# Four prepared half tiles instead of three in the block phase of a hybrid decoder layer, with the forget gate kept in DRAM meanwhile

## The chip, the core and the metric

The kernel runs on one core of one Trainium2 chip. The metric is the device time of one execution in microseconds; the time before is the median of three runs. Engines are named as in the profile: PE is the matrix engine (PEld its weight loads), DVE the vector engine, ACT the scalar engine, POOL the GpSimd engine, SP the engine that here only issues DMAs. POOL also issues DMAs, on a queue of its own.

## What is computed

One decoder layer of width 2048 on 256 tokens. A normalised input is multiplied by one wide matrix, whose columns feed two mixers in parallel: a gated linear attention (GLA) with four heads and a differential attention with sixteen. Both outputs are gated, projected, merged and projected once more. Cut to what matters:

```
h = rmsnorm(x, pre_norm_g)
a_q, a_k, a_v, a_g, a_lr, b_q, b_k, b_v, b_g, m_a, m_b = split(h @ w_in)
gk  = log_sigmoid(a_lr @ gla_gk_w2 + gla_gk_b) / 16          # the forget gate
o_a = gla_chunked(a_q, a_k, a_v, gk)                          # needs gk
y_a = (rmsnorm(o_a) * silu(a_g)) @ w_branch_a
o_b = diff_attention(b_q, b_k, b_v, lam)
y_b = (0.8 * rmsnorm(o_b) * silu(b_g)) @ w_branch_b
x   = x + rmsnorm((sigmoid(m_a) * y_a + sigmoid(m_b) * y_b) @ w_out)
```

All of it is float32. A product of two float32 matrices is made of three products of rounded parts: each operand is split into a high part (rounded) and a low part (the rest), and hi by hi, hi by lo and lo by hi are summed.

## The kernel before, in words

**Half tiles.** The weights come from DRAM in the order in which they are used, and are taken in half tiles of 128 x 1024 values (4 KB a partition). For each half, `emit_half` (L339) makes two tiles: `hi`, a rounding copy by ACT (L371), and `lo`, the raw values minus hi, by DVE (L372). Both lie in a pool with three buffers each (`wpool`, L148, tags `hi` and `lo`). `take` (L380) hands the next pair to the matmuls, and first sees to it that the halves up to three further (`AHEAD`, L24) have been emitted. A tile of the fourth half from here takes the buffer of the present one, and so waits until PE has used it.

**The phase.** After the v columns 2 to 3 of GLA (`token_major`, L594) comes the phase (L920 to L931). Its order is written out by `phase_steps` (L102): ten block sets, of seven products each in the order `PRODUCTS` (1, 3, 2, 5, 6, 7, 4), and every product in four halves: 28 halves a set. A set is a 2 x 2 block product with seven multiplications instead of eight, so its weights are sums of blocks. Two blocks of each set are loaded into `chain` tiles (`link`, L222) and changed in place: DMAs on POOL's queue add blocks to them (L252), and DVE adds b or c to a (L260). The third kind of raw block, `c` (named `raws`), is loaded by SP into the big pool (L241, L242), four tiles a set. Between the products of a set lie partner halves of other weights (`PARTNERED`, L38, and four more in the first set): the last v columns, then q and k of GLA, then the first heads of the differential attention. A set's half is six matmuls for PE, a partner's half twelve or sixteen. PE's order in the phase is the program's own (`mm`, L578). SP's and POOL's DMAs are pinned to program order as well (`tc.keep_in_program_order`), while ACT and DVE instructions are ordered by the framework's planner.

**What leaves a product.** After product 6 and product 7 of a set DVE reads the bank into a tile `gr` (L901, L910, with raised priority), after 2 and 4 ACT writes a tile `gl` (L864, L868). Both are stored to DRAM by POOL (`spill`, L174) in the next set, at its product 3 (`SPILL_AT`, L40).

**The big pool.** `u` (L158) hands out its 18 buffers of 4 KB a partition (`BIG`, L42). In the phase it holds the eight tiles of the normalised input (`xs`, L390), the c tiles, gr and gl, a tile of q or k in the making, v tiles until they are stored, and the two tiles `gp` of the forget gate (L665). These are made while the v columns 2 and 3 are multiplied (`forget_gate`, L644; the last step is L687) and first read after the phase, in `gla_scores` (L944, the exponential at L967 of the profile). A buffer whose tile is stored comes free when the store has landed.

**The end of the phase.** When product 7 of the last set begins its second quarter, POOL fetches q and k of both halves back into the big pool (L927, L928). After the phase, the chain tiles' memory becomes a second pool (L934), and GLA is worked on beside the remaining heads.

## Time and profile before

| | |
|---|---|
| runs shown, median (lowest to highest) | 1079.25 us (1079.2 to 1079.81) |
| profiled execution | 1080.03 us |
| its span, first to last instruction | 1078.1 us |
| mean granted PE clock | 0.999 |
| DMA traffic | 295.54 MB, mean 274 GB/s |
| phase, from its first matmul to the end of the last set's partner | 81.3 to 633.9 us, and products 4 of the last set behind it |

The profile is of one execution. A row of a group of instructions gives the line of the kernel, the engine, the operation, what it writes and reads, its count, then the busy time and the mean of one in ns, then the idle time of the engine before them and what ended it. A row of the timeline gives start and duration in us, engine, line, operation, and in brackets the idle time just before it with its releaser. A row of a stretch gives its bounds, its length, the busy time of each engine (with the number of its instructions), PE's granted clock, the mean busy share of the 16 DMA engines and the GB/s. A row of waits reads: who waited, for whom, total us, times, longest. PE's end times are modelled, as matmuls overlap.

### The profile page before, as it was taken

The numbers are of one execution on the slowest core, as the hardware profiler recorded it, in microseconds if no ns is written. First come the engines' busy times: TensorE is split into PE (matmuls) and PEld (weight loads), VectorE is DVE, ScalarE is ACT, GpSimd is POOL, SyncE is SP. The second block draws the span as 40 slices with busy tenths as digits, with TensorE's granted clock in tenths as the row PEclk, the third lists the DMA queues.
The fourth block names the chain that finished last, engine by engine and source line by source line (L and its number), as shares of the span: only waits on it lengthen the run. The fifth ranks groups of instructions, "written<-read, shape, count | busy, mean of one in ns | idle before, by whom it ended". The sixth has DMA issues, their size and how long they took to land.

```text
span 1078.1 us, 15451 instructions
## 1 busy us (share of the span) xinstructions
PE 1066.4 (99%) x5380; PEld 914.4 (85%) x5380; DVE 959.7 (89%) x1273; ACT 765.3 (71%) x1122; POOL 179.6 (17%) x259
## 2 busy tenths in 40 slices
PE   9999999999999999999999999999999999999997
PEld 8998888888888888888888888898988888888886
DVE  7798999999999999999999989976877988889886
ACT  7897676777676767676767766765687887566662
POOL 0201121212121212121212211012111112100000
PEclk9999999999999999999999999999999999999999
DMA  9899798989898989999898867769989888988752
GB/s 349 271 352 310 194 339 259 322 230 320 224 324 215 310 245 335 284 273 303 267 298 262 206 231 279 253 206 310 334 282 305 264 269 273 346 303 257 271 192 99
DMA packets 68365, 295.54 MB, mean 274 GB/s; under 512 B 8832, under 2 KB 11904, under 8 KB 51648
## 3 DMA queue, kind: packets, MB, share of 16 engines
q1 hardware_dynamic: 38080, 167.99, 43.8%
q0 software_dynamic: 29632, 125.84, 42.6%
q8 instruction: 42, 0.69, 0.3%
q10 hardware_dynamic: 576, 0.73, 0.2%
q14 instruction: 35, 0.29, 0.1%
HBM read 267.27 MB, written 27.26 MB: 273 GB/s over the span
## 4 chain that ended last, share of the span: by engine, by line
PE 82%; DVE 7%; issue 5%; ACT 2%; DMA 2%; POOL 1%; POOLq 0%; SPq 0%; DVEq 0%; ACTq 0%
PE mm L579 55%; PE bg L579 20%; DVE lo L372 3%; PE mm L567 2%; PE bg L567 2%; DMA vback<-vl 1%; PE mm L552 1%; DVE a L260 1%; ACT prob L1158 1%; ACT hi L371 1%; DMA raw<-in_w_dram 0%; DVE prob L1152 0%; PE bg L1172 0%; PE bg L1064 0%; PE bg L1364 0%
## 5 line engine op out<-in xcount | busy, mean ns | idle before, releaser
L371 ACT ACTIVATE hi<-raw 128x1024 fp32r<-128x1024 f32 (+3 forms) x213 | 217.0, 1025 | 117.0 <-PE bg L579 51.7
L372 DVE TENSOR_TENSOR lo<-raw,hi 128x1024 fp32r<-128x1024 f32 (+3 forms) x215 | 251.8, 1177 | 39.7 <-ACT hi L371 36.8
L371 ACT ACTIVATE hi<-a 128x1024 fp32r<-128x1024 f32 x160 | 169.3, 1061 | 53.7 <-PE mm L579 35.3
L372 DVE TENSOR_TENSOR lo<-a,hi 128x1024 fp32r<-128x1024 f32 x160 | 190.6, 1220 | 6.3 <-ACT hi L371 4.4
L579 PE MATMUL mm<-hi,xs 128*128 128x512 f32 (+1 forms) x608 | 155.8, 382 | 0.0
L579 PEld LDWEIGHTS mm<-hi,xs 128*128 128x128 f32 x608 | 114.0, 188 | 18.5
L579 PE MATMUL bg<-xs,hi 128*128 128x512 f32 x448 | 115.4, 390 | 0.0
L372 DVE TENSOR_TENSOR lo<-b,hi 128x1024 fp32r<-128x1024 f32 x80 | 97.8, 1223 | 12.3 <-ACT hi L371 9.9
L579 PEld LDWEIGHTS bg<-xs,hi 128*128 128x128 f32 x448 | 84.2, 188 | 16.4
L371 ACT ACTIVATE hi<-b 128x1024 fp32r<-128x1024 f32 x80 | 84.2, 1059 | 19.2 <-PE mm L579 17.3
L579 PE MATMUL mm<-lo,xs 128*128 128x512 f32 (+1 forms) x304 | 88.6, 381 | 0.0
L579 PE MATMUL mm<-xs,hi 128*128 128x512 f32 x320 | 82.2, 394 | 0.0
L252 POOL DMA_DIRECT2D b<-in_w_dram x40 | 34.9, 873 | 204.7 <-DVE a L260 123.1
L579 PEld LDWEIGHTS bg<-xs,lo 128*128 128x128 f32 x448 | 60.9, 190 | 6.9 <-DVE lo L372 2.8
L579 PEld LDWEIGHTS mm<-xs,hi 128*128 128x128 f32 x320 | 57.4, 189 | 9.9
L579 PEld LDWEIGHTS mm<-lo,xs 128*128 128x128 f32 x304 | 57.0, 188 | 9.7
L579 PE MATMUL bg<-xs,lo 128*128 128x256 f32 x448 | 62.8, 283 | 1.5 <-DVE lo L372 1.5
L372 DVE TENSOR_TENSOR lo<-c,hi 128x1024 fp32r<-128x1024 f32 x40 | 49.0, 1226 | 5.5 <-ACT hi L371 1.4
L579 PE MATMUL mm<-hi,oah 128*128 128x512 f32 x128 | 50.9, 397 | 1.3 <-DVE part L1334 1.3
L371 ACT ACTIVATE hi<-c 128x1024 fp32r<-128x1024 f32 x40 | 42.5, 1062 | 11.8 <-PE mm L579 10.9
L579 PE MATMUL mm<-hi,oal 128*128 128x512 f32 x128 | 50.1, 391 | 0.0
L260 DVE TENSOR_TENSOR a<-a,b 128x1024 f32<-128x1024 f32 x40 | 48.8, 1221 | 0.6
(408 smaller groups left out, 2283.9 us busy)
## 6 DMA issues: line engine op xcount, KB each, us to landing
raw<-in_w_dram SPq DMA_DIRECT2D x90, 1024.0 KB, 7.6
c<-in_w_dram SPq DMA_DIRECT2D x40, 512.0 KB, 6.9
a<-in_w_dram POOLq DMA_DIRECT2D x40, 512.0 KB, 9.5
b<-in_w_dram POOLq DMA_DIRECT2D x40, 512.0 KB, 8.3
a<-in_w_dram POOLq DMA_DIRECT2D x18, 1024.0 KB, 15.9
b<-in_w_dram POOLq DMA_DIRECT2D x18, 1024.0 KB, 9.8
raw<-in_w_dram SPq DMA_DIRECT2D x14, 832.0 KB, 7.8
gr<-gr POOLq DMA_DIRECT2D x10, 512.0 KB, 13.3
```

Of the source, the lines that this page charges most:

```text
L252: tc.keep_in_program_order(pool.dma_start(chain[s, name, i][:, c], block(s, 1, i)[:, c], accum_op=ALU.add))
L260: add = dve.tensor_tensor(out=a, in0=a, in1=chain[s, "b", i][:, c] if second else raws[s, i, h], op=ALU.add)
L371: act.activation(hi_t[:, a:b], r[:, a:b], AF.Copy)
L372: dve.tensor_tensor(out=lo_t[:, a:b], in0=r[:, a:b], in1=f32(hi_t[:, a:b]), op=ALU.subtract)
L552: i = pe.matmul(out, lhs, rhs, start=first and n == 0, stop=last and n == len(pairs) - 1, **kw)
L567: i = pe.matmul(banks[g][b][:, :n], a[part][:, P * b : P * b + P], w[:, n * g : n * g + n], start=first, stop=last)
L579: i = pe.matmul(*args, **kw)
L1158: act.activation(prob[m][:, lo:up], prob[m][:, lo:up], AF.Exp, scale=score_scale[:, b : b + 1], bias=mx[:, i : i + 1], accum_out=z[:, i : ...
```

## The change

Within the phase, four halves are prepared ahead instead of three. Every fourth half emitted there, counted from the first one, has its hi and lo tiles in the big pool and not in the three buffers. The two gp tiles are stored to DRAM by POOL when the forget gate is done, and fetched by POOL into the big pool with q and k, so the order of the six fetches is q, k, gp of the first half and q, k, gp of the second. Before the phase and after it, three halves are prepared ahead as before.

```diff
@@ -22,6 +22,7 @@
 RANK = 16
 AHEAD = 3
+PHASE_AHEAD = 4
 LANES = 3
@@ -326,6 +327,7 @@
     joint_loads = [False]
+    joined_stage = [0]
     alive = [0]
@@ -355,6 +357,8 @@
             hi_t, lo_t = make([P, 1024], "keep", F32R), make([P, 1024], "keep", F32R)
+        elif joined_stage[0] and (j - joined_stage[0]) % 4 == 3:
+            hi_t, lo_t = u([P, 1024], "hi", F32R), u([P, 1024], "lo", F32R)
         else:
@@ -380,7 +384,7 @@
         used[0] += 1
-        while emitted[0] < min(j + 1 + AHEAD, len(seq)):
+        while emitted[0] < min(j + 1 + (PHASE_AHEAD if joined_stage[0] else AHEAD), len(seq)):
             emit_half()
@@ -685,6 +689,7 @@
             dve.scalar_tensor_tensor(out=z[hf], in0=z[hf], scalar=0.0, in1=e[hf], op0=ALU.min, op1=ALU.subtract)
+        gp[:] = [spill(t, "gp") for t in gp]
         done.add("gate")
@@ -920,16 +925,20 @@
     pinned[0] = joint_loads[0] = True
+    joined_stage[0] = emitted[0]
     fetched = []
@@
         if step == ("set", SETS - 1, 7, 1, 0):
-            fetched = [[fetch(ts[name, hf], name, u) for name in ("q", "k")] for hf in range(2)]
+            for hf in range(2):
+                fetched.append([fetch(ts[name, hf], name, u) for name in ("q", "k")])
+                gp[hf] = fetch(gp[hf], "gp", u)
         next(sets if step[0] == "set" else rest)
@@
     pinned[0] = joint_loads[0] = False
+    joined_stage[0] = 0
     joint.close()
```

## The prediction

> **What bounds the kernel now.** I read the page first, for the shares of the engines, and then cut the span at the ten block sets of the phase, because the change works there.

> ```profile
> span 1078.1 us, 15451 instructions
> PE 1066.4 (99%) x5380; PEld 914.4 (85%) x5380; DVE 959.7 (89%) x1273; ACT 765.3 (71%) x1122; POOL 179.6 (17%) x259
> ```

> ```profile
> core 0: us, PE busy (x) PEld busy (x) DVE busy (x) ACT busy (x) POOL busy (x), PEclk, DMA share, GB/s
> 81.32:138.82 57.50, 56.79 (x274) 49.37 (x273) 51.70 (x53) 40.14 (x46) 10.55 (x15) 1.00 0.92 263
> 138.82:193.66 54.84, 54.84 (x266) 46.30 (x265) 52.49 (x52) 39.91 (x43) 10.28 (x14) 1.00 0.94 301
> ...
> 413.02:468.45 55.43, 55.10 (x266) 46.21 (x265) 52.56 (x50) 40.37 (x44) 11.89 (x17) 1.00 0.97 299
> 468.45:523.29 54.84, 54.84 (x265) 46.30 (x265) 53.05 (x52) 40.45 (x44) 11.36 (x16) 1.00 0.96 290
> 523.29:579.05 55.76, 55.10 (x266) 46.22 (x265) 53.56 (x53) 40.79 (x45) 12.55 (x18) 1.00 0.89 263
> ```

> PE is busy for 99% of the span. Undisturbed sets take 54.84 us with PE busy for all of it, at granted clock 1.00; DVE has 52.49 to 53.05 us of work in them. So PE sets the pace and DVE follows with about 2 us to spare. Only two later sets are longer: 55.43 - 54.84 = 0.59 us and 55.76 - 54.84 = 0.92 us; the first has gaps of its own. The PE timeline shows what it waited for there.

> ```profile
> 134.51 0.73 PE L579 MATMUL mm<-lo,r3h 128*128 128x512 f32 x2 [0.20 <-DVE lo L372]
> ...
> 137.38 1.21 PE L579 MATMUL bg<-xs,lo 128*128 128x256 f32 x8 [0.52 <-DVE lo L372]
> ...
> 467.01 1.21 PE L579 MATMUL bg<-xs,lo 128*128 128x256 f32 x8 [0.33 <-DVE lo L372]
> ...
> 577.61 0.62 PE L579 MATMUL bg<-xs,lo 128*128 128x256 f32 x3 [0.66 <-DVE lo L372]
> ```

> All four waits are for the same thing, the low part of a half tile. The idle time shown is 0.26 us less than what its set lost (0.33 against 0.59, 0.66 against 0.92), since matmul ends are modelled; with 0.26 added to each, the first set lost 0.46 + 0.78 = 1.24 us. All lookahead stalls together are 1.24 + 0.59 + 0.92 = 2.75 us. That is the most that more lookahead can give in the phase.

> Is DVE late for want of speed, or was it held back earlier? The waits from 139 to 634 us, and the timeline rows of ACT and DVE ahead of the last stall:

> ```profile
> ACT hi L371 <- PE mm L579: 61.1, 165, 0.8
> ACT hi L371 <- PE bg L579: 59.1, 54, 2.0
> ...
> PE bg L579 <- DVE lo L372: 1.0, 2, 0.7
> ```

> ```profile
> 562.55 1.06 ACT L371 ACTIVATE hi<-b 128x1024 fp32r<-128x1024 f32 x1 [0.82 <-PE mm L579]
> ```

> ```profile
> 563.65 1.22 DVE L372 TENSOR_TENSOR lo<-b,hi 128x1024 fp32r<-128x1024 f32 x1 [0.62 <-ACT hi L371]
> ...
> 576.34 1.22 DVE L372 TENSOR_TENSOR lo<-raw,hi 128x1024 fp32r<-128x1024 f32 x1
> ```

> ACT stood 120 us waiting for PE to give back a hi tile. At 562.55 it got one, DVE had idled 0.62 us for it, and then DVE worked without a gap up to the lo at 576.34 that PE was missing. So DVE was held back by the three tiles, 14 us before the stall. It idled 57.50 - 51.70 = 5.80, 2.87 and 2.20 us in the three sets, more than each stall.

> **The change, part by part.** *One half tile more.* It lets DVE do one lo more (1.22 us) before the heavy stretch. The stalls of 0.59 and 0.92 us are below that and go; of the 1.24 us about 0.02 stays. Gain 2.75 us, between 1.8 (only 0.62 of idle is used ahead of each of the two longer stalls: 0.59 + 0.62 + 0.62) and 2.75. I take 2.75, as the idle in each set is larger than the stall. ACT and DVE do the same number of instructions, and what is late next is nothing: outside these places PE has no gap in the phase. The bank reads after products 6 and 7 keep their raised priority, so the extra half in front of them costs nothing.

> *The two stores.* They wait for the two L687 instructions, on POOL's queue.

> ```profile
> L687 DVE SCALAR_TENSOR_TENSOR gp<-gp,e x2: 1219/1222/1224, 69.7 to 72.9; 128x1024 f32<-128x1024 f32 x2
> ```

> ```profile
> 68.06 0.53 POOL L177 DMA_DIRECT2D vl<-vl  x1
> 79.92 0.91 POOL L252 DMA_DIRECT2D a<-in_w_dram  x1 [11.32 <-DVE lo L372]
> ```

> L687 ends at 70.9 and 74.1, and POOL idles 11.32 us from 68.6 to 79.9, so two issues of 0.53 us delay nothing on that queue. Their 1.05 MB meet the loads, though. Below, from the DMA view of single issues: the time to landing of the vl store of 68.06 and of the next one, 16 us later; then three stretches of DMA share; then the raw load of 81.16, the one that is needed soonest, and the ACT and PE instructions that use it.

> ```profile
> vl<-vl POOLq DMA_DIRECT2D x1, 512.0 KB, 12.6
> ```

> ```profile
> vl<-vl POOLq DMA_DIRECT2D x1, 512.0 KB, 16.2
> ```

> ```profile
> 76.00:80.00 4.00, 4.00 (x23) 3.96 (x23) 3.72 (x5) 3.42 (x4) 0.08 (x1) 1.00 0.79 298
> 80.00:84.00 4.00, 4.00 (x20) 3.52 (x19) 4.00 (x6) 3.24 (x7) 2.30 (x4) 1.00 0.81 170
> ...
> 88.00:92.00 4.00, 4.00 (x22) 3.66 (x21) 2.69 (x3) 3.06 (x4) 0.71 (x2) 1.00 1.04 306
> ```

> ```profile
> raw<-in_w_dram SPq DMA_DIRECT2D x1, 800.0 KB, 12.7
> ```

> ```profile
> 93.95 0.87 ACT L371 ACTIVATE hi<-raw 128x800 fp32r<-128x800 f32 x1 [0.56 <-DMA raw<-in_w_dram]
> ```

> ```profile
> 96.69 0.52 PE L579 MATMUL bg<-hi,xs 128*128 128x400 f32 x2
> ```

> At 306 GB/s the stores take 3.4 us of all DMA engines. From 76 to 84 us 0.21 x 4 + 0.19 x 4 = 1.6 us are free; 1.8 us push the loads of the full stretch. The raw load then lands 1.8 us later; ACT would be ready at 94.82 + 1.8 = 96.6, and PE asks at 96.69. So it costs from 0 to 3.4 - 1.87 = 1.5 us; I take 0.4, near the row.

> [...]

> *The fetches.* Two more, behind those of q and k of each half, in the last set. First the landing of the q fetches, in the window from 617 to 626 us, then the first reader of gp.

> ```profile
> q<-q POOLq DMA_DIRECT2D x2, 512.0 KB, 6.4
> ```

> ```profile
> L967 ACT ACTIVATE decay<-gp x2: 1044/1052/1059, 649.2 to 650.1; 128x1024 f32<-128x1024 f32 x2
> ```

> Six fetches of 6.4 us from 617 on end at 636 with two in flight at a time, as now, and at 655 one after another; the reader comes at 649.2. I take 0; the bound is a wait of 6 us on ACT, with the next hi tiles queued behind it and PE waiting for those.

> The sum: -2.75 + 0.4 = -2.35 us. The profiled execution (1080.03 us, span 1078.1) would become 1077.7; the median of the runs shown, 1079.25, becomes **1076.9**. A change of 0.2% (2.2 us) is about what a measurement of this kernel can tell from no change.

> **The rivals.** *Slots that are still being stored.* The big pool is full in the phase; the weight queue's own waits say so, and stores land late:

> ```profile
> SPq L242 <- DVE a L260: 138.3, 21, 18.1
> SPq L242 <- DMA gl<-gl: 113.3, 7, 29.6
> ```

> ```profile
> gr<-gr POOLq DMA_DIRECT2D x10, 512.0 KB, 13.3
> gl<-gl POOLq DMA_DIRECT2D x10, 512.0 KB, 14.0
> ```

> ```profile
> 138.82 21.78 PE mm L579 x96
> 160.60 2.77 PE bg L579 x16
> ```

> Today c loads on SP wait for such slots and nobody minds. After the change hi and lo tiles, every fourth half, ask for slots of the same pool. If one is handed the slot of a gl or gr tile whose store is in flight, ACT stops in order until it lands. Asked right at the issue, the half is ready after 14.0 + 1.06 + 1.22 = 16.3 us; PE gets there after four halves of 1.36 us (the 96 matmuls above are 16 halves) and a partner of 2.77, 8.2 us. That is a stall of up to 8 us in each of nine sets; asked half way, 7.0 + 2.3 - 8.2 = 1.1, and with the lead of 1.2 us gone, 2.3. Nine times 2.3 is 21 us: 1098 us, with 1081 to 1120 as bounds. It decides from 2.35/9 = 0.26 us a set. For it: L242 waited 113.3 us on gl stores. Against it: two slots are freed for two tiles, and the older, free slot may be the one given.

> *The weight queue at the start.* SP issues the four c loads of set 0 and then the raw loads in a fixed order, and the last c loads already wait for a store:

> ```profile
> 69.50 11.56 SPq L242 DMA_DIRECT2D c<-in_w_dram  x4
> 81.16 22.47 SPq L311 DMA_DIRECT2D raw<-in_w_dram  x4
> ```

> ```profile
> SPq L242 <- DMA vl<-vl: 2.2, 1, 2.2
> ```

> If the fourth c load gets gp's slot instead, it waits until 74.1 + 12.6 = 86.7, and the raw load moves from 81.16 to 87. With the same 12.7 us it lands 5.8 us later and PE stalls 5.8 - 1.87 = 3.9 us; with a queue that has drained meanwhile, 1. That gives 1077.9 to 1080.8, no change.

> *No effect.* DVE's order shifts and the stalls stay, 1079.3. Against it stands the idle time of DVE in all three sets.

> [...]

> **How the numbers follow.** Forecast 0.50, its own range 1075.9 to 1079.0 (gain 1.8 to 2.75, cost 0 to 1.5, 0.6 for what moves behind the phase): 0.37 of it beyond 0.2%. Slots in flight 0.27, of it 0.26 slower. Weight queue 0.16, of it 0.02 slower. No effect 0.07. Faster 0.37; same 0.13 + 0.01 + 0.14 + 0.07 = 0.35; slower 0.28. The range is 1075.9 to 1088: it holds the forecast, the queue and the slot case up to about 1.2 us a set, and leaves out some 0.18, nearly all above.

> **What would show it.** Right: all sets but the first at 54.84 us, no PE wait for lo in the phase, ACT's wait for PE shorter than 120 us, the raw load landing before 96. Wrong: ACT or DVE waiting for a DMA of gl, gr, gp or vl in the phase (slots), set lengths above 54.84 in a row, a raw wait of ACT near 94 us of 2 us or more (queue), or the same three stalls (no effect).

## The result, and the profile after

The changed kernel takes 1118.86 us (median of four runs, 1115.2 to 1120.53), the kernel before 1079.22 us beside it: a ratio of 1.0362 (95% interval 1.0342 to 1.0382), 39.6 us slower. The forecast was 1076.9, its range ended at 1088.

First the head of the profile's page of the changed kernel:

```profile
span 1117.8 us, 15381 instructions
PE 1078.6 (96%) x5380; PEld 919.2 (82%) x5380; DVE 953.6 (85%) x1273; ACT 756.1 (68%) x1122; POOL 182.4 (16%) x263
```

The number of matmuls is the same, 5380, but PE is busy for 1078.6 us instead of 1066.4, and idle for 39.2 instead of 11.7. The stretches show where. They begin at the phase's first matmul and end with the span; first the kernel before, then the changed one (columns as in the table of stretches above: bounds, length, PE, PEld, DVE, ACT, POOL, clock, DMA share, GB/s):

```profile
81.32:633.96 552.64, 550.93 (x2650) 465.96 (x2649) 525.57 (x503) 402.83 (x439) 110.61 (x155) 1.00 0.92 275
633.96:1078.10 444.14, 436.60 (x2316) 372.93 (x2314) 368.24 (x666) 294.20 (x564) 59.29 (x88) 1.00 0.80 264
```

```profile
81.03:673.38 592.35, 562.09 (x2651) 470.91 (x2651) 520.59 (x504) 394.91 (x440) 112.09 (x157) 0.98 0.87 259
673.38:1117.80 444.42, 437.12 (x2316) 372.71 (x2314) 366.74 (x666) 293.12 (x563) 59.53 (x88) 1.00 0.81 264
```

All of it lies in the phase: 592.35 - 552.64 = 39.7 us; behind it the two kernels differ by 0.3. Of the 39.7, PE's idle time grew from 1.71 to 30.26 us (28.5), and its busy time for the same work by 11.2, at a mean clock of 0.98. Cut at the same matmuls as in the prediction, the sets of the changed kernel are:

```profile
81.03:140.09 59.06, 56.76 (x275) 49.42 (x274) 52.88 (x54) 40.32 (x47) 10.54 (x15) 1.00 0.91 271
140.09:196.98 56.89, 55.74 (x266) 46.13 (x265) 51.53 (x51) 38.88 (x43) 10.32 (x14) 1.00 0.89 272
...
253.97:319.51 65.54, 57.81 (x266) 48.35 (x264) 51.44 (x49) 38.92 (x43) 10.79 (x15) 0.92 0.83 252
319.51:381.85 62.34, 57.09 (x266) 47.70 (x264) 52.85 (x52) 39.15 (x43) 10.85 (x15) 0.95 0.77 220
381.85:449.21 67.36, 58.60 (x266) 48.16 (x264) 51.12 (x48) 38.69 (x43) 10.23 (x14) 0.92 0.80 242
...
618.08:673.38 55.30, 55.12 (x266) 46.29 (x265) 51.48 (x51) 39.10 (x44) 12.45 (x18) 1.00 0.92 271
```

Three sets carry 31 of the 39.7 us (54.84 would be undisturbed), and these three have the low clock. Now the waits of the changed kernel from 81 to 680 us (who waited for whom, total, times, longest):

```profile
ACT hi L375 <- PE mm L583: 70.7, 108, 3.0
...
ACT hi L375 <- PE bg L583: 27.0, 26, 2.6
DVE lo L376 <- DMA gr<-gr: 26.0, 3, 9.8
PE mm L583 <- DVE lo L376: 25.1, 7, 7.7
...
PE mm L583 <- DVE gr L906: 3.6, 4, 2.2
```

ACT's wait for PE to give back a hi tile is shorter, as forecast: 70.7 + 27.0 = 97.7 us, against 69.2 + 64.1 = 133.3 us in the kernel before (from 81 to 636 us). But DVE waits for the store of gr: three times, 26.0 us. That is the first rival of the prediction. The longest of these, in the timeline of DVE and then of PE (start, duration, engine, line, operation, idle time before it with its releaser):

```profile
268.24 2.54 DVE L376 TENSOR_TENSOR lo<-c,hi 128x1024 fp32r<-128x1024 f32 x2 [0.41 <-ACT hi L375]
280.54 1.23 DVE L376 TENSOR_TENSOR lo<-raw,hi 128x1024 fp32r<-128x1024 f32 x1 [9.76 <-DMA gr<-gr]
281.68 1.22 DVE L376 TENSOR_TENSOR lo<-c,hi 128x1024 fp32r<-128x1024 f32 x1
```

```profile
274.15 1.07 PE L583 MATMUL mm<-hi,xs 128*128 128x512 f32 x4
282.95 1.22 PE L583 MATMUL mm<-lo,xs 128*128 128x512 f32 x2 [7.73 <-DVE lo L376]
```

Look twice. PE stops at a product of a c half, and goes on when the lo made from c at 281.68 is done. The lo that waited for gr's store was made from raw, for the partner's half that PE uses next. So the half that met the store was not the one that PE needed: it stood in front of it on DVE. The planner had put it there. (The second of the three waits has the same pattern: a lo of an a half waits until 343.59, and PE goes on at 346.01, when the lo of a c half behind it is done.)

And behind the stall, the stretch of the wait and the next 6 us:

```profile
274.00:282.90 8.90, 1.22 (x6) 0.68 (x4) 2.36 (x3) 0.96 (x1) 0.00 (x0) 0.76 0.93 369
282.90:288.90 6.00, 5.95 (x18) 4.98 (x19) 5.97 (x6) 3.75 (x4) 0.92 (x1) 0.51 0.31 39
```

For 6 us the granted clock is 0.51. So a stall of 7.7 us costs some 3 us more.

### The profile page after: what moved, and what is told of

Read it like the earlier page. It is cut to its first block, busy times and chain, and to the rows that moved or that the text cites. A ratio compares the mean times of both kernels' runs of the same rounds, so it can differ in the third digit from the quotient of the medians.

```text
span 1117.8 us, 15381 instructions
## 1 busy us (share of the span) xinstructions
PE 1078.6 (96%) x5380; PEld 919.2 (82%) x5380; DVE 953.6 (85%) x1273; ACT 756.1 (68%) x1122; POOL 182.4 (16%) x263
## 4 chain that ended last, share of the span: by engine, by line
PE 51%; DVE 3%; ACT 2%; issue 1%; DMA 1%; POOL 0%; POOLq 0%; DVEq 0%; ACTq 0%
PE mm L583 35%; PE bg L583 11%; DVE lo L376 1%; PE bg L1022 1%; PE mm L556 1%; DMA a<-in_w_dram 1%; PE bg L556 1%; ACT prob L1167 1%; ACT hi L375 0%; DVE prob L1161 0%; PE bg L1181 0%; PE bg L1073 0%; PE bg L1373 0%; PE bg L1155 0%; PE bg L1156 0%
## 5 line engine op out<-in xcount | busy, mean ns | idle before, releaser
L375 ACT ACTIVATE hi<-a 128x1024 fp32r<-128x1024 f32 x160 | 166.5, 1057 | 108.0 <-PE mm L583 36.0
L583 PE MATMUL bg<-xs,hi 128*128 128x512 f32 x448 | 120.2, 402 | 0.0
L583 PEld LDWEIGHTS bg<-xs,hi 128*128 128x128 f32 x448 | 87.7, 196 | 17.8
L376 DVE TENSOR_TENSOR lo<-c,hi 128x1024 fp32r<-128x1024 f32 x40 | 48.3, 1222 | 3.7 <-ACT hi L375 2.7
## 6 DMA issues: line engine op xcount, KB each, us to landing
c<-in_w_dram SPq DMA_DIRECT2D x40, 512.0 KB, 7.9
a<-in_w_dram POOLq DMA_DIRECT2D x40, 512.0 KB, 11.1
b<-in_w_dram POOLq DMA_DIRECT2D x40, 512.0 KB, 6.6
gr<-gr POOLq DMA_DIRECT2D x10, 512.0 KB, 15.3
```

The lines of the kernel that those rows point to most:

```text
L375: act.activation(hi_t[:, a:b], r[:, a:b], AF.Copy)
L376: dve.tensor_tensor(out=lo_t[:, a:b], in0=r[:, a:b], in1=f32(hi_t[:, a:b]), op=ALU.subtract)
L583: i = pe.matmul(*args, **kw)
```

## The experiments

All comparisons are with the kernel before, on the same chip. "Phase" and "behind it" are the two stretches as above; in the kernel before they take 552.64 and 444.14 us.

**The parts of the change alone.** e2_gate_store_only keeps the stores and fetches of gp and undoes the rest:

```
-PHASE_AHEAD = 4
+PHASE_AHEAD = 3
...
-        elif joined_stage[0] and (j - joined_stage[0]) % 4 == 3:
-            hi_t, lo_t = u([P, 1024], "hi", F32R), u([P, 1024], "lo", F32R)
```

> Only the storing and fetching of the forget gate's tiles is kept: three halves ahead, hi and lo in their ring as in the kernel before. The big pool has two buffers free in the phase. Theory (slots): the cost of the stores alone is 0 to 1.5 us, so 1079.2 to 1080.8, with the stalls of the kernel before still there. Rival (weight queue at the start: the fourth c load of set 0 waits for the gate's store until 83.5 us and the raw loads behind it start 2.8 us later): up to 1082, with a PE stall near 97 us. A time under 1078.5 would say that the two freed buffers are worth something by themselves.

```profile
81.47:634.12 552.65, 550.95 (x2651) 465.74 (x2650) 525.37 (x503) 402.91 (x439) 111.75 (x157) 1.00 0.93 278
```

Ratio 1.0004 (0.9995 to 1.0013); the phase is unchanged to 0.01 us. The stores and fetches cost nothing.

e3_slots_no_lookahead keeps the big pool for every fourth half but not the fourth half ahead (PHASE_AHEAD = 3 alone).

> As the changed kernel, with every fourth half in the big pool, but only three halves ahead in the phase. Theory (slots): each half asks for its buffer one half (1.36 us and more) later, so the waits for gr, gl, q and k remain and the stalls are as long or longer: 1110 to 1135. Rival B (the lookahead is what costs): 1079 to 1083. Rival A (late bank reads): those 3.6 us go, the rest stays.

It took 1131.2 us, ratio 1.0475 (1.046 to 1.049). So the time is lost by giving these tiles buffers of the pool, not by the longer lookahead; the lookahead makes the loss 12 us smaller.

e1_own_ring keeps the lookahead and takes hi and lo out of the big pool:

```
-BIG = 18
+BIG = 16
...
-        elif joined_stage[0] and (j - joined_stage[0]) % 4 == 3:
-            hi_t, lo_t = u([P, 1024], "hi", F32R), u([P, 1024], "lo", F32R)
...
-            hi_t = wpool.tile([P, 1024], F32R, tag="hi", name=f"hi_{j}")
+            hi_t = wpool.tile([P, 1024], F32R, tag="hi", name=f"hi_{j}", bufs=4)
```

(and lo likewise).

> The lookahead stays four and the forget gate's tiles are still stored, but the fourth hi and lo tiles are two more buffers of their own ring (four of each) and the big pool has 16 buffers instead of 18, so no hi or lo can be given a buffer whose store is in flight. Theory (slots: the change is slow because every fourth half is given a big-pool buffer that a store still reads; 21.1 us of PE idle in three stalls that DVE spends waiting for gr, some 7 us in smaller ones, some 8 us of lower granted clock behind the long ones): all waits of ACT and DVE for gr, gl, q and k are gone, no stretch has a clock below 0.99, time 1077 to 1081. Rival A (late bank reads: four halves ahead put lo instructions before the bank read after product 6, PE waits for gr L906 3.6 us in four places): these 3.6 us stay, so it ends at the upper end, 1080 to 1082. Rival B (the longer lookahead itself, or DMA traffic, is what costs 39.6 us): 1110 to 1120.

```profile
80.95:630.97 550.02, 550.02 (x2650) 466.00 (x2649) 524.97 (x504) 402.89 (x439) 111.75 (x157) 1.00 0.94 280
630.97:1082.40 451.43, 439.61 (x2316) 375.32 (x2314) 366.47 (x665) 293.68 (x563) 61.95 (x88) 0.99 0.79 259
```

The phase is without a gap: PE busy for 550.02 of 550.02 us, 2.62 less than before. All 42 us between it and the changed kernel's phase are gone, and so are the late bank reads, so rivals A and B fall as causes of their own. The whole kernel is still slower, 1084.23 us, ratio 1.0040 (1.0025 to 1.0054), above the 1077 to 1082 us of the theory and of rival A: behind the phase it loses 7.3 us, which neither had counted. The waits from 631 us on show 5.3 of them:

```profile
PE mm L581 <- DVE part L1341: 5.3, 2, 2.9
```

The next two kernels put the two extra buffers into the chain tiles' pool (tags of one buffer each, for every fourth half), so that the memory goes over to the second pool after the phase (MORE = 18); the second also fetches the part tiles there.

> As e1_own_ring, but the two extra buffers lie in the chain tiles' pool, whose memory goes over to the second pool after the phase (18 buffers there instead of 16); the big pool keeps 16. e1 ended the phase 2.99 us ahead of the kernel before and lost 7.2 us behind it, in two waits of PE for the bank read of part (L1341) of 2.5 and 3.1 us. Theory (buffers of the big pool are short behind the phase too): the second pool doesn't hold part, so the two waits stay: 1083 to 1085. If the second pool's two buffers take work off the big pool's: 1077 to 1080.

> As e5_ring_given_back, and the four part tiles are fetched into the second pool. Theory (the 7.2 us behind the phase are the two buffers that the big pool lacks there): the waits for part shrink to the 0.66 and 0.99 us of the kernel before or below, the phase keeps its 2.6 to 3.0 us: 1076 to 1078. Rival (the late bank reads come from the longer lookahead or the order, not from buffers): 1083 to 1085.

Both have a phase of 550.2 us, and take 1080.59 and 1080.85 us, ratios 1.0010 (1.0001 to 1.0019) and 1.0011 (1.0002 to 1.0020). PE's waits for part are back to 1.4 and 1.3 us (1.3 in the kernel before), in the first also, where that was not expected: its big pool has 16 buffers, as in e1, so that number alone is not what made part late there. Some 3.7 us behind the phase stay lost in other places. Both times miss their expectations; how the pools' sizes act behind the phase was not followed further.

**When the stores land.** e4_stores_earlier (SPILL_AT = (1, 0, 0) instead of (3, 0, 0)):

> As the changed kernel, but POOL stores gr and gl at product 1 of the next set instead of product 3, four halves (about 5.4 us) earlier, and ahead of a chain load of 1 MB on its queue. Theory (slots): the stores land at least 5.4 us earlier against the halves that ask for the buffers; the three stalls of 7.9, 5.4 and 7.8 us shrink to 2.5, 0 and 2.4 and the lower clock behind them goes, some 24 us less: 1088 to 1100. If the cost has nothing to do with when the stores land: within 3 us of 1118.9.

It took 1129.11 us, ratio 1.0452 (1.0435 to 1.0468), 10 us more than the changed kernel, and fits neither expectation. The edit moved the stores in the program, but hardly in time. POOL's timeline of the fourth set, which begins at 262.2 us here:

```profile
269.82 0.85 POOL L253 DMA_DIRECT2D a<-in_w_dram  x1 [0.49 <-DVE lo L376]
270.37 0.86 POOL L178 DMA_DIRECT2D gr<-gr  x1
```

The store stands behind accumulating loads that wait for lo, and is issued 8.1 us into the set; in the changed kernel it was 8.7. e6_stores_by_act takes it off that queue: settle_owed stores by `act.dma_start`, and the planner places the issue behind ACT's last write of each tile.

> As the changed kernel, but gr and gl are stored by ACT right behind its own last write of them, and not by POOL behind the chain loads in its queue. e4_stores_earlier had moved the stores in the program but not in time: they were still issued 10 us into the set, since POOL's queue stood at accumulating loads that wait for lo. Theory (slots: it is the store in flight that holds the buffer): gr is stored some 9 us and gl some 3 us earlier and outside that queue, the three stalls of 7.9, 5.4 and 7.8 us and the clock loss of 2 to 3 us behind each go: 1086 to 1096. If the time of landing isn't what holds hi and lo: 1115 to 1122.

The DMA view (KB each, median us to landing) of the changed kernel, and then of this one:

```profile
gr<-gr POOLq DMA_DIRECT2D x10, 512.0 KB, 15.3
gl<-gl POOLq DMA_DIRECT2D x10, 512.0 KB, 16.0
```

```profile
gr<-gr ACTq DMA_DIRECT2D x10, 512.0 KB, 9.0
gl<-gl ACTq DMA_DIRECT2D x10, 512.0 KB, 8.7
```

The stores land in little more than half the time, and PE's longest wait for lo falls from 7.7 to 2.0 us, as expected. The total does not: 1118.78 us, ratio 1.0366 (1.0331 to 1.0400). PE's waits in its phase:

```profile
PE mm L586 <- ACT hi L378: 8.9, 8, 3.0
PE mm L586 <- DVE lo L379: 8.7, 13, 2.0
PE mm L586 <- DVE gr L909: 4.2, 4, 2.6
```

Many short waits have taken the place of three long ones. That fits a wait whose length is set by the store's landing; but the theory that the landing makes the whole cost failed here. One thing blurs the test. The buffers are handed out anew in each build, and by the addresses in the built programs 19 of the 172 hi and lo tiles in the pool come right behind a gr or gl tile in e6, against 12 in the changed kernel.

e8_stores_own_buffers takes gr and gl out of the big pool (`blocks.tile(..., tag="gr", bufs=1)` and gl likewise; BIG = 16, MORE = 18) and leaves hi and lo in it.

> The fourth hi and lo tiles stay in the big pool, as in the changed kernel, but gr and gl are made in one buffer each of their own (in the chain tiles' pool; the big pool has 16 buffers, the second pool 18). So hi and lo can still meet the stores of q, k, vh and vl, and the c tiles, but never those of gr and gl, and the stores keep their place in POOL's queue. Theory (slots, and of these the gr and gl stores above all): waits for gr and gl vanish, those for q and k (2 to 4 us each, four times) stay; the phase, 592.4 us in the changed kernel and 552.7 in the one before, takes 552 to 562; behind the phase some 3.4 us are lost to the pools' sizes as in e5_ring_given_back. Time 1080 to 1091. Rival (e6_stores_by_act took the long stalls away and still ended at 1118.8: sharing the pool costs by the order of the pool's buffers whatever tile is met): over 1105.

1136.19 us, ratio 1.0520 (1.0489 to 1.0551): the worst of all. There is no hi or lo that waits for gr or gl, and 605.6 us of phase; it lies where the rival expected it. Two faults of the edit blur it: gl's single buffer makes ACT wait, in some sets up to 3.3 us, for gl's own last store, and the last c load of the first set now waits for vl's store until 93.5 us, with the raw loads behind it, which alone stops PE for 8.8 us. With the half clock behind that stop, and gl's waits counted in full (8.5 us of ACT), this is some 20 of the 53 us that the phase has lost. Where the rest comes from isn't separated. The trace does show ACT waiting 53.5 us for chain loads of a and b (30.9 and 22.6), against 8.8 in the changed kernel and none in the one before.

**The order.** In the kernel before and in e1_own_ring ACT makes every hi in the order in which PE uses the halves. In the changed kernel 170 of 523 hi tiles come behind one that PE uses later, in e6 147 and in e8 187: halves of the big pool are put ahead of their turn, most often by three places. (This is counted in the built programs.) e10_order_kept pins the order in the changed kernel:

```
+            keep = tc.keep_in_program_order if joined_stage[0] else lambda i: i
             if j:
-                act.activation(hi_t[:, a:b], r[:, a:b], AF.Copy)
+                keep(act.activation(hi_t[:, a:b], r[:, a:b], AF.Copy))
```

(and lo likewise).

> The changed kernel with its order of work pinned: in the phase ACT makes the hi tiles and DVE the lo tiles in the order in which PE uses them. Without the pin the planner puts many halves of the big pool up to three places ahead of halves that PE needs sooner; at 274.8 us PE waits for a lo that has nothing to do with the big pool and stands on DVE behind the lo that waits for gr's store. Theory (slots alone: the wait for the store sets the time, the order is an accident): 1110 to 1122. Theory (order alone: a pool half made too early blocks the halves needed sooner, and in its own place its store would have landed): phase 552 us, 1079 to 1083. Both: the long stalls shrink from 7.9, 5.4 and 7.8 us by some 3 us each (two matmuls of the stalled half, then the eight hi matmuls of the partner come first), those under 3 us go with the clock loss behind them: 1088 to 1105.

1104.28 us, ratio 1.0224 (1.0207 to 1.0240), 14.6 us less than the changed kernel. Phase and PE's waits in it:

```profile
81.82:660.89 579.07, 559.76 (x2650) 468.19 (x2650) 522.21 (x503) 392.94 (x439) 111.66 (x157) 0.99 0.89 265
```

```profile
PE mm L584 <- DVE gr L907: 18.2, 8, 3.4
PE mm L584 <- DVE lo L377: 1.0, 2, 0.8
PE bg L584 <- DVE lo L377: 0.8, 1, 0.8
```

The time lies where "both" was expected, but by another way than that: PE hardly waits for lo any more (25.1 us without the pin, 1.8 with it), although DVE and ACT still wait for stores of gr, gl, k and q; and the bank read behind product 6 comes late instead, eight times. DVE's timeline at one of them:

```profile
244.74 1.23 DVE L261 TENSOR_TENSOR a<-a,c 128x1024 f32<-128x1024 f32 x1
245.88 1.23 DVE L377 TENSOR_TENSOR lo<-raw,hi 128x1024 fp32r<-128x1024 f32 x1
247.01 0.69 DVE L907 TENSOR_TENSOR gr<-mm,p 128x512 f32<-128x512 f32 x1
```

PE stands from 245.06 to 247.85 while DVE works off lo and a + c first. Why the planner puts the read so far back here, and not in e1, was not tried.

> As e8_stores_own_buffers (gr and gl in buffers of their own, hi and lo of every fourth half still in the big pool), with the order pinned as in e10_order_kept. e8 had no hi or lo waiting for gr or gl and was 56.6 us slower than the kernel before all the same. Theory (order is the second cause): 1080 to 1092, with waits for q, k, vh and vl left and some 3.4 us behind the phase from the pools' sizes. If the order doesn't matter: 1130 to 1140.

e11 (e8 with that pin): 1126.46 us, ratio 1.0432 (1.0418 to 1.0447), 10 us less than e8 and far from what was expected. The wait for gl's own buffer (up to 5.1 us of ACT a set) and the 9.6 us at the start are in it, so it tells little more than that the order has a share there too.

**Held buffers.** e9_held_buffers takes the two big-pool buffers once and keeps them for the phase.

> As the changed kernel in everything (big pool of 18, the forget gate stored and fetched, four halves ahead, every fourth half in two big-pool buffers), but the two buffers are taken once at the phase's start and held to its end, written by each fourth half in turn, and not handed back and asked for anew. Theory (the fault is the asking, not the two buffers or the pool): phase 550 us as in e1_own_ring, 436 us behind it as in the kernel before: 1076 to 1078. Rival (the pool is short of two buffers whoever holds them, and c tiles come late): over 1082.

It took 1125.47 us, ratio 1.0425 (1.0409 to 1.0440), but it doesn't test this: the next fourth half was written ahead of the present one's matmuls, so that every fourth half multiplied the wrong weights and waited for them. e12_held_in_turn emits the next one behind them:

```
-            hi_t, lo_t = u([P, 1024], "hi", F32R), u([P, 1024], "lo", F32R)
+            hi_t, lo_t = held
...
+            if held and (emitted[0] - joined_stage[0]) % 4 == 3 and emitted[0] - joined_stage[0] > 3 and emitted[0] - 4 >= j:
+                break
             emit_half()
...
+    held[:] = [u([P, 1024], "hi", F32R), u([P, 1024], "lo", F32R)]
```

> As e9_held_buffers, whose fault is mended: there the next fourth half was written, in the program's order, before the matmuls of the present one, so these multiplied the wrong weights and waited for them. Here the next one is emitted behind the present one's matmuls. All else as the changed kernel: big pool of 18, the forget gate stored and fetched, four halves ahead, every fourth half in two big-pool buffers that are held for the phase. Theory: phase 550 us as in e1_own_ring and e5, 436 us behind it as in the kernel before: 1076 to 1078. Rival (the pool is short of buffers for c whoever holds the two): over 1082.

```profile
81.72:632.45 550.73, 550.13 (x2651) 466.02 (x2651) 525.18 (x504) 403.74 (x440) 111.77 (x157) 1.00 0.94 279
632.45:1076.80 444.35, 436.64 (x2316) 372.83 (x2314) 366.13 (x665) 293.32 (x563) 59.56 (x88) 1.00 0.80 263
```

1078.61 us, ratio 0.9990 (0.9981 to 0.9999): the fastest version, by 1.9 us in the phase and with 0.2 lost behind it; 0.6 above the expected range. (The "436 us behind it" of the two expectations is PE's busy time there, 436.60 us; the stretch is 444.14 long in the kernel before.) Pool, stores and fetches are those of the changed kernel, and so is the lookahead, but for the fourth halves themselves: each is emitted when the one before it has been used, three ahead of PE. What differs besides, by 40 us, is that two buffers are taken once, and not asked for anew by each of the 86 fourth halves. That removes three things together: tiles beyond two, meetings with stored tiles, and the changed order of work, since ACT's order is PE's again.

**The clock.** e7_idle_doses lets PE stand in the kernel before, with ACT repeating a copy and no store or buffer involved.

> The kernel before, with ACT repeating one rounding copy (the same values written again) 5, 7, 9, 11 and 14 times ahead of product 5 in sets 1, 3, 5, 6 and 8, so that PE stands idle for growing times, some 0 to 11 us, with no store or buffer involved. Theory (PE's idle time itself brings the clock down: in the runs so far idle times from 2.4 to 10.3 us were followed by 3 to 6 us at a granted clock of 0.5, worth 1.7 to 2.9 us, and those up to 2.3 us by nothing): each stall of over 2.5 us is followed by a stretch of clock 0.5 that costs 1.7 to 2.9 us, whatever its length; the shorter ones by none. Rival (the slow matmuls behind a stall are short of weights or buffers, or belong to the stores): full clock and no loss beyond the idle time here.

PE's five waits were 4.1 to 13.8 us, so all were above 2.5. The stretches of the shortest and of the fourth, each with what follows:

```profile
163.00:167.10 4.10, 0.07 (x1) 0.00 (x0) 0.00 (x0) 4.05 (x5) 0.00 (x0) 0.93 1.00 417
167.10:169.40 2.30, 2.27 (x5) 1.82 (x6) 2.29 (x3) 0.15 (x1) 0.00 (x0) 0.50 0.77 264
...
464.00:474.90 10.90, 0.33 (x3) 0.12 (x2) 0.01 (x1) 10.64 (x11) 0.00 (x0) 0.63 0.42 154
474.90:480.00 5.10, 5.09 (x12) 4.04 (x13) 5.10 (x5) 1.47 (x2) 0.00 (x0) 0.50 0.02 3
```

Each was followed by 2.8 to 5.8 us of work at a clock of 0.50. PE's busy time in the phase rose from 550.93 to 564.17 us, 2.6 a stall; the half clock accounts for 1.4 to 2.9 us of a stall, as expected but for the shortest. So the idle time itself lowers the clock, with no store or buffer involved. In the changed kernel PE works 5.89, 4.27 and 5.95 us at half clock behind the three stalls, 16.1 us together. Half of that, 8 us, is what the clock costs there, most of the 11.2 us of longer busy time; the other 3 us were not followed.

## Why the prediction was wrong

**The gain, right.** The three stalls were to go and give 2.75 us, between 1.8 and 2.75. Where hi and lo have buffers of their own the phase is 2.62 (e1), 2.45 (e5) and 1.91 us (e12) shorter. That DVE was held back by the three buffers was the right reading.

**The stores and fetches, right.** 0.4 us was taken for the stores; e2 shows 0.0. The fetches were taken at nothing: behind the phase 444.42 against 444.14 us.

**The weight queue, right in kind.** In the changed kernel the fourth c load of the first set waits 8.6 us for gp's store, and the raw load behind it is issued at 83.96 instead of 81.16 us. It lands 10.1 us later instead of 12.7, so at 94.06 instead of 93.86, hardly later. PE loses 0.26 us there, because ACT makes another c half first, at 94.79, and the hi of raw only at 95.75. In e12 the same place costs PE 0.6 us, a part of what e12 lacks against e1.

**The slots: the step that failed.** The prediction named this rival, the place and the sign by which it would be known, and then gave it 0.27 because "two slots are freed for two tiles, and the older, free slot may be the one given". Both parts of that failed. The phase has 280 halves of the sets and 64 of the partners, so 86 fourth halves with two tiles each: 172 requests, and the program binds each to one buffer before it runs. By the addresses in the built program they lie in ten buffers of the pool, not in two. With the times of the trace, three or four of these tiles are in use at once for 303 us of the phase, since four halves ahead the next fourth half is made while PE still uses the present one. And 21 of the 172 come right behind a tile on its way out (gl 8, gr 4, vl 3, q 2, k 2, vh 1, gp 1). The first long stall is one of them: gr's store is issued at 262.66, and the lo in the same buffer is written at 280.54. Counted beforehand, this would have spoken against a chance of 0.27, and against ending the range at 1088.

**Its price, too low.** 2.3 us in each of nine sets gave 1098. It came as three stalls of 7.7, 5.3 and 7.6 us, within the "up to 8 us" named for one stall, and small change elsewhere; what met gr's stores was lo on DVE, where the prediction had hi on ACT. Two things were not in the sum. One is the order: the half that waits stands in front of halves that PE needs sooner, so the lead of four halves doesn't protect PE (the pin of e10 takes 14.6 us off). The other is the clock behind the long stalls: 8 us.

**"The bank reads cost nothing", half right.** With four halves ahead in buffers of their own PE never waits for gr. In the changed kernel it does for 3.6 us, and in e10 for 18.2: the raised priority didn't hold the place of the read there.

**What stays open.** e3, e1 and e12 show that taking these tiles anew from the shared pool is the cause of the 40 us, and e10 that the order of work is a share of it. How the rest divides isn't settled, because e1 and e12 each remove the meetings with stores, the tiles beyond two and the changed order together. Tiles beyond two are not all of it: in e10 three are in use at once for only 20 us, and the kernel is still 24 us slower. e6 shortens the waits for stores and e8 takes those for gr and gl away, and neither is faster. The c loads, which ask the same pool, start later in these kernels (the first of the fourth set 10.3 us ahead of the set in the changed kernel, 28.0 in the one before). But in the trace of the changed kernel no engine is seen waiting for a c load, so that they carry the rest is not shown.

## What to carry to other kernels

Before a short-lived tile moves into a shared pool, count its requests, count how many of it can be alive at once, and list what else leaves that pool by DMA; spare buffers don't help if each request is bound to one buffer ahead of time. Give such a tile its own buffers, or hold two of the pool's for the whole stage, as e12 does; here even that gained only 0.1%. Where one tile's wait holds up the tiles behind it, as the lo made from c stood on DVE until 281.68 behind the one that waited 9.76 us, look at which half PE stopped for and which half the engine was waiting with: if they differ, the order is a cause beside the wait.

## What was not expected of the hardware

**The clock after a stall.** That PE's clock falls behind a stall was in no part of the prediction. The traces show more of it than the rows of 0.50 and 0.51. The stretches at half clock last 3.41, 6.83, 10.24 or 13.65 us between 20 and 1060 us in every trace that has some, which is one to four times 3.41. Within a trace they all begin and end on one raster of that step, whenever the wait began: in the changed kernel they run from 278.60 to 288.84, from 343.45 to 350.28 and from 408.30 to 418.54, and the starts are 64.85 us apart, 19 steps of 3.413. PE need not stand for a whole step. Below is e4 around a wait of 2.20 us (126.99 to 129.19), cut at that raster, and then e10 around a wait of 3.24 us (360.58 to 363.82):

```profile
126.52:129.93 3.41, 1.21 (x6) 0.81 (x5) 3.41 (x4) 3.36 (x5) 1.06 (x2) 1.00 0.62 199
129.93:133.34 3.41, 3.41 (x9) 2.65 (x8) 3.41 (x5) 1.14 (x2) 0.54 (x1) 0.50 0.86 286
```

```profile
358.85:362.26 3.41, 1.73 (x12) 1.34 (x10) 3.41 (x4) 0.38 (x1) 0.56 (x1) 1.00 0.01 2
362.26:365.67 3.41, 1.84 (x8) 1.58 (x9) 2.37 (x5) 1.90 (x3) 0.55 (x1) 1.00 0.91 329
365.67:369.08 3.41, 3.41 (x20) 2.90 (x19) 3.41 (x4) 2.73 (x3) 0.00 (x0) 1.00 0.78 296
```

**The queue of a store.** The same 512 KB stores took 15.3 and 16.0 us to land when POOL issued them behind its loads (the changed kernel), and 9.0 and 8.7 us when ACT issued them (e6). They were also issued at other times, so how much of this is the queue isn't separated.
